# The first pair of a GeGLU MLP: x in pieces of 256 tokens by half of K, first half of K for all tokens first

## The chip, the cores and the metric

The kernel runs on one core of a Trainium2 chip. The time is the device time of one execution in microseconds (us); the traces place an instruction to some 0.1 us. TensorE is the matrix engine (PE in the profile, its weight loads PEld), VectorE is DVE, ScalarE is ACT, GpSimd is POOL; SPq is the queue on which SyncE issues the transfers.

## The reference

```python
# x: (8, 1024, 1024), w_gate, w_up: (1024, 4096), w_down: (4096, 1024), all fp32
gate = x @ w_gate
up = x @ w_up
gate = 0.5 * gate * (1 + tanh(sqrt(2 / pi) * (gate + 0.044715 * gate ** 3)))
out = (gate * up) @ w_down
```

## The kernel before

The kernel handles 1024 tokens at a time in eight passes, in fp16, with Strassen-like schemes of fewer products. In pass 0 nothing is prepared yet, so the first pair of column blocks (two blocks of 128 columns of gate and of up) is computed plainly: x is loaded in fp32, cast by VectorE, transposed by TensorE into PSUM, and copied out into four operands b11, b21 (first 512 tokens, two halves of K) and b12, b22 (the other 512 tokens). `mh` is the half of the tokens, `kh` the half of K, `g` a block of 128 tokens. Each load of x or of a weight block is 512 KB.

```python
def x0_load(mh, g):                       # 128 tokens, all of K: rows of 4 KB
    r0 = mh * MH + g * P
    nc.sync.dma_start(out=x0_f32[mh][:, g], in_=x2[r0 : r0 + P, :])

def x0_transpose(mh, g, b):
    ...                                   # eight 128x128 transposes into PSUM bank b
    nc.vector.tensor_copy(xq["b11" if mh == 0 else "b12"][:, :, c], ps[:, 0:KH])
    ...                                   # the other half of K is copied by ScalarE
# order of the loads:  x (mh 0) x4, weights of pair 0 x4, x (mh 1) x4, weights of pair 1 x4
...
def first_pair():
    ...
    warm(9)                               # matmuls on ones, to bring the clock up
    ...                                   # transposes of mh 0, each followed by warm(2) or warm(3)
    for kh in range(2):
        products(0, kh, slice(0, MH))
    ...                                   # casts and transposes of mh 1, first 256 tokens
    for kh in range(2):
        products(1, kh, slice(0, MQ))
    ...                                   # transposes of mh 1, other 256 tokens
    for w in range(2):
        cast_first(w, 1, slice(256, 512)) # last weight block of pair 1, on ScalarE
    for kh in range(2):
        products(1, kh, slice(MQ, MH))
    ...
    sum_x(1); sum_w(0, 1, 0); sum_w(0, 1, 1); sum_x(2)     # VectorE, for pair 1
    outputs(1, 0); outputs(1, 1)
    sum_x(3); sum_w(0, 1, 2); sum_w(0, 1, 3); sum_x(4)
```

Pair 1 is the next one. It starts with four products that need only x and its own weights (16 matmuls) and goes on with products of the sums.

## Time and profile before

| what | us | where it is read |
|---|---|---|
| median of six runs (2256.08 to 2257.9) | 2256.44 | times |
| span of the profiled run | 2254.4 | page |
| TensorE busy | 2246.1 | page, part 1 |
| first product of the first pair | 11.47 | timeline |
| first matmul of pair 1 | 28.72 | timeline |
| pair 1 comes to its last four products | 39.10 | timeline |
| last first-pair load lands | 27.3 | issue plus time to landing |
| wait of the matmuls at 279.69 | 0.43 | waits of TensorE |

A line of the timeline gives the start, the duration, the engine, the line of the program, the operation with what it writes and reads, how many instructions were merged, and in brackets how long the engine was idle before it and what ended that. Line numbers differ between the kernels: the first pair's products are L1198 before and L1206 after, pair 1 is L626 before and L635 after, the down projection L991 and L1000.

### The profile page before, as it was taken

How to read it: one execution, taken by the hardware profiler on the slowest of the kernel's cores; microseconds unless marked ns; L12 is line 12 of the kernel's file. 1: busy time of each engine (PE TensorE's matmuls, PEld its weight loads, DVE VectorE, ACT ScalarE, POOL GpSimd, SP SyncE). 2: the span in 40 equal slices, each digit the busy share in tenths (PEclk: the TensorE clock that was granted, in tenths of full speed). 3: DMA queues.
4: the chain of work that ended last, by engine and by line, in shares of the span. 5: the costliest groups of instructions: out<-in, count | busy, mean ns of one | idle time of the engine just before them, and what ended most of it. 6: DMA issues, size and time to landing. Idle time of an engine off the chain costs nothing.

```text
span 2254.4 us, 42805 instructions
## 1 busy us (share of the span) xinstructions
PE 2246.1 (100%) x16634; PEld 1625.6 (72%) x16634; DVE 1561.7 (69%) x2190; ACT 956.1 (42%) x1866; POOL 679.3 (30%) x825
## 2 busy tenths in 40 slices
PE   9999999999999999999999999999999999999999
PEld 4444444444444445888888888888888888888888
DVE  6576458883588755777776677666786667866674
ACT  4444135651355622666125550356404653055520
POOL 1332013330133200555014550255403543044520
PEclk9999999999999999999999999999999999999999
DMA  9898969989999999999998999989999889988876
GB/s 241 163 207 218 284 184 241 263 264 283 255 227 249 282 309 349 328 342 370 302 339 274 317 304 318 322 270 324 311 324 316 285 308 326 311 311 277 289 285 225
DMA packets 308093, 642.46 MB, mean 285 GB/s; under 512 B 79088, under 2 KB 185328, under 8 KB 287344
## 3 DMA queue, kind: packets, MB, share of 16 engines
q1 hardware_dynamic: 253104, 566.57, 73.2%
q0 software_dynamic: 54784, 73.14, 19.3%
q8 instruction: 130, 2.13, 0.4%
q14 instruction: 75, 0.61, 0.1%
HBM read 574.36 MB, written 138.41 MB: 316 GB/s over the span
## 4 chain that ended last, share of the span: by engine, by line
PE 87%; DMA 2%; SPq 0%; DVE 0%; issue 0%; DVEq 0%
PE ps L848 40%; PE ps L1099 20%; PE ps L626 17%; PE ps L991 10%; DMA wd_quads<-x_sums 1%; SPq L255 0%; DMA ring<-wd_ops 0%; DVE x_sums L452 0%; DVE h_a L923 0%; DVE tmp L1168 0%; DVE x_sums L278 0%; SPq L487 0%; DVEq L278 0%; SPq L535 0%
## 5 line engine op out<-in xcount | busy, mean ns | idle before, releaser
L848 PEld LDWEIGHTS <-ring 128*128 128x128 f16 x8320 | 814.1, 98 | 94.4
L825 POOL TENSOR_TENSOR h_a<-tmp 128x256 f16<-128x256 f32 x640 | 469.3, 753 | 839.3 <-ACT tmp L813 831.9
L848 PE MATMUL ps<-x_sums,ring 128*128 128x256 f16 x5760 | 655.8, 273 | 0.0
L810 DVE TENSOR_TENSOR tmp<-tmp,ps 128x512 f32<-128x512 f32 x640 | 414.5, 683 | 148.1 <-PE ps L848 99.7
L626 PEld LDWEIGHTS <-ring 128*128 128x128 f16 x2632 | 257.5, 98 | 310.4
L795 ACT COPY tmp<-ps 128x512 f32<-128x512 f32 x520 | 304.1, 585 | 237.5 <-PE ps L848 162.8
L626 PE MATMUL ps<-x_sums,ring 128*128 128x512 f16 x1504 | 339.8, 379 | 0.0
L813 ACT ACTIVATE tmp<-tmp 128x256 f32<-128x256 f32 x640 | 264.1, 418 | 172.8 <-DVE tmp L808 79.4
L848 PE MATMUL ps<-x_b,ring 128*128 128x256 f16 x2560 | 305.6, 273 | 0.0
L808 DVE TENSOR_TENSOR tmp<-ps,tmp 128x512 f32<-128x512 f32 x240 | 165.4, 689 | 145.2 <-ACT tmp L795 101.0
L626 PE MATMUL ps<-x_b,ring 128*128 128x512 f16 x1128 | 259.1, 379 | 0.0
L652 POOL TENSOR_TENSOR h_a<-tmp 128x512 f16<-128x512 f32 x94 | 144.5, 1537 | 374.8 <-ACT tmp L650 271.9
L1099 PEld LDWEIGHTS <-h_a 128*128 128x128 f16 x2240 | 219.2, 98 | 25.4
L991 PE MATMUL ps<-ring,h_a 128*128 128x512 f16 x1024 | 222.3, 379 | 0.4 <-DMA ring<-wd_ops 0.4
L1099 PE MATMUL ps<-ring,h_a 128*128 128x256 f16 x1920 | 216.1, 273 | 0.0
L991 PEld LDWEIGHTS <-h_a 128*128 128x128 f16 x1152 | 112.7, 98 | 136.6 <-DMA ring<-wd_ops 0.9
L645 DVE TENSOR_TENSOR tmp<-ps,tmp 128x512 f32<-128x512 f32 x188 | 127.2, 683 | 112.6 <-ACT tmp L637 111.1
L1156 ACT ACTIVATE tmp<-ps 128x512 f32<-128x512 f32 x60 | 35.3, 597 | 362.6 <-PE ps L1099 274.6
L1168 DVE SCALAR_TENSOR_TENSOR tmp<-ps,tmp 128x512 f32<-128x512 f32 x120 | 81.1, 690 | 97.5 <-PE ps L1099 66.6
L351 DVE TENSOR_TENSOR ring<-ring 128x1024 f16<-128x1024 f16 x188 | 138.7, 751 | 11.1 <-DMA ring<-in_w_up_dram 6.9
L637 ACT COPY tmp<-ps 128x512 f32<-128x512 f32 x188 | 109.9, 586 | 77.8 <-PE ps L626 77.8
L1099 PE MATMUL ps<-ring,x_sums 128*128 128x256 f16 x1120 | 126.3, 273 | 0.0
(102 smaller groups left out, 1532.0 us busy)
## 6 DMA issues: line engine op xcount, KB each, us to landing
ring<-w_ops SPq DMA_DIRECT2D x480, 512.0 KB, 5.0
ring<-wd_quads SPq DMA_DIRECT2D x110, 1024.0 KB, 7.0
ring<-wd_ops SPq DMA_DIRECT2D x35, 1024.0 KB, 8.2
out_dram<-tmp SPq DMA_DIRECT2D x128, 256.0 KB, 6.6
w_ops<-h_s SPq DMA_DIRECT2D x128, 256.0 KB, 6.7
ring<-in_w_gate_dram POOLq DMA_DIRECT2D x23, 1024.0 KB, 10.5
ring<-in_w_up_dram POOLq DMA_DIRECT2D x23, 1024.0 KB, 17.8
wd_quads<-x_sums SPq DMA_DIRECT2D x131, 128.0 KB, 6.4
```

What stands on the lines that cost most here:

```text
L351: nc.vector.tensor_tensor(o, a, b, op)
L626: nc.tensor.matmul(ps(b, w), lhs[:, k], rhs[:, k, :], start=(first and k == 0), stop=(k == KH - 1), skip_group_check=True,)
L645: nc.vector.tensor_tensor(o, ps("b", w), o, ADD)
L652: nc.gpsimd.tensor_tensor(hq[TO[n]][:, i, :], tmp[:, t[n, 1]], tmp[:, t[n, 0]], MUL)
L795: nc.scalar.copy(tmp[:, t[o[1]]], ps_all[:, bank[o[2]]])
L808: nc.vector.tensor_tensor(d, b, a, SUB)
L810: nc.vector.tensor_tensor(d, a, b, ADD if o[4] == "add" else SUB)
L813: nc.scalar.activation(d, d, GELU, scale=GSC)
L825: nc.gpsimd.tensor_tensor(h, tmp[:, t[o[1]], MQ : 2 * MQ], g, MUL)
L848: nc.tensor.matmul(ps_all[:, bank[c], w * MQ : (w + 1) * MQ], lhs[:, w, k], rhs[:, k], start=(first and w == 0 and k == 0), stop=(k == KH ...
L991: nc.tensor.matmul(ps_all[:, bank[b, g]], lhs[:, j, g * P : (g + 1) * P], dc[:, n, :], start=(first and j == 0), stop=(j == NP - 1), skip_ ...
L1099: nc.tensor.matmul(ps_all[:, bank[c], m * MQ : (m + 1) * MQ], lhs[:, j, m * P : (m + 1) * P], rhs[:, j, :], start=(first and j == 0 and m ...
```

## The change

The intent is to let TensorE begin real work earlier. x comes in pieces of 256 tokens by half of K, the first half of K for all tokens before the second, so that the first products need two pieces of x and one weight block instead of four and one. The transposes go through spare PSUM banks, the PSUM copies become one instruction of 1024 elements per piece, the first gate casts are split in two, and the warm-up shrinks from 18 matmuls to 12.

```diff
-    def x0_load(mh, g):
-        r0 = mh * MH + g * P
-        nc.sync.dma_start(out=x0_f32[mh][:, g], in_=x2[r0 : r0 + P, :])
+    def x0_load(mh, gp, kh):
+        r0 = mh * MH + gp * MQ
+        nc.sync.dma_start(
+            out=x0_piece(x0_f32[mh], gp, kh),
+            in_=x2[r0 : r0 + MQ, kh * KH * P : (kh + 1) * KH * P].rearrange("(t p) k -> p t k", p=P),
+        )
 ...
-        warm(9)
 ...
+        warm(7)
+        x0_cast(0, 0, 0)
+        x0_cast(0, 1, 0)
+        x0_transpose(0, 0, 0, 4, act)
+        warm(2)
+        x0_transpose(0, 1, 0, 5, dve)
+        warm(3)
+        halves(0)
+        cast_first(1, 0, c0, dve)
+        product(0, 0, 0, 0)
+        product(0, 0, 0, 1)
+        product(0, 0, 1, 0)
 ...          (the other pieces in the same manner)
+        for c in (lo, hi):
+            for w, j in ((0, 0), (0, 1), (1, 0)):
+                product(1, 1, w, j, c)
         for kh in range(2):
-            products(1, kh, slice(MQ, MH))
-
+            product(1, kh, 1, 1)
+        cast_first(0, 1, c1)
+        cast_first(1, 1, c1, dve)
         ps_free.clear()
-        ps_free.extend((0, 2, 1, 3, 4, 5, 6, 7))
+        ps_free.extend(range(8))
         sum_x(1)
 ...
+    for kh in range(2):
+        for gp in range(2):
+            x0_load(0, gp, kh)
+        for w in range(2):
+            load_first(w, kh, slice(0, 256))
+        for gp in range(2):
+            x0_load(1, gp, kh)
 ...          (then the four weight blocks of pair 1, as before)
```

More of the change, by code (lines that the diff above doesn't have):

```diff
@@ L290, with x0_piece, x0_cast, x0_transpose @@
     x0_f16 = hf["a12"].rearrange("p (t a) -> p t a", t=2 * G)
-    def x0_load(mh, g):
-        r0 = mh * MH + g * P
-        nc.sync.dma_start(out=x0_f32[mh][:, g], in_=x2[r0 : r0 + P, :])
-    def x0_cast(mh, g):
-        nc.vector.tensor_scalar(x0_f16[:, mh * G + g], x0_f32[mh][:, g], XSC, None, MUL)
-    def x0_transpose(mh, g, b):
-        h = x0_f16[:, mh * G + g]
-        ps = ps_all[:, b].bitcast(FP16).rearrange("p (k m) -> p k m", m=P)
-        for k in range(2 * KH):
-            nc.tensor.transpose(ps[:, k], h[:, k * P : (k + 1) * P], identity)
-        c = slice(g * P, (g + 1) * P)
-        nc.vector.tensor_copy(xq["b11" if mh == 0 else "b12"][:, :, c], ps[:, 0:KH])
-        if mh:
-            nc.scalar.copy(xq["b22"][:, :, c], ps[:, KH : 2 * KH])
-        else:
-            return lambda: nc.scalar.copy(xq["b21"][:, :, c], ps[:, KH : 2 * KH])
+    def x0_piece(t, gp, kh):
+        return t[:, 2 * gp : 2 * gp + 2, kh * KH * P : (kh + 1) * KH * P]
+    def x0_load(mh, gp, kh):
[4 more added lines that the diff above has]
+        )
+    def x0_cast(mh, gp, kh):
+        nc.vector.tensor_scalar(
+            x0_piece(x0_f16, 2 * mh + gp, kh), x0_piece(x0_f32[mh], gp, kh), XSC, None, MUL
+        )
+    def x0_transpose(mh, gp, kh, b, copy):
+        h = x0_piece(x0_f16, 2 * mh + gp, kh)
+        ps = ps_all[:, b].bitcast(FP16).rearrange("p (k m) -> p k m", m=MQ)
+        o = xq[f"b{kh + 1}{mh + 1}"][:, :, gp * MQ : (gp + 1) * MQ]
+        for k in range(KH):
+            for t in range(2):
+                nc.tensor.transpose(
+                    ps[:, k, t * P : (t + 1) * P], h[:, t, k * P : (k + 1) * P], identity
+                )
+        copy(o, ps)
     def raw(p, q):
@@ L328, in load_first, with cast_first @@
         )
-    def cast_first(w, kh, cols, copy=nc.scalar.copy):
-        copy(raw(0, 0)[:, w, kh * KH : (kh + 1) * KH, cols], staging0(w, kh)[:, :, cols])
+    def cast_first(w, kh, cols, copy=nc.scalar.copy, ks=slice(0, KH)):
+        o = raw(0, 0)[:, w, kh * KH : (kh + 1) * KH, cols]
+        copy(o[:, ks], staging0(w, kh)[:, ks, cols])
     def load_raw(p, q):
@@ L1192, in first_pair, with product @@
         bank = {(mh, j, w): 4 * mh + 2 * j + w for mh in range(2) for j in range(2) for w in range(2)}
-        def products(mh, kh, c):
-            for w in range(2):
-                for j in range(2):
-                    for k in range(KH):
-                        nc.tensor.matmul(
-                            ps_all[:, bank[mh, j, w], c],
-                            raw(0, 0)[:, w, kh * KH + k, j * P : (j + 1) * P],
-                            xq[f"b{kh + 1}{mh + 1}"][:, k, c],
-                            start=(kh == 0 and k == 0 and c.start == 0),
-                            stop=(kh == 1 and k == KH - 1),
-                            skip_group_check=True,
-                        )
+        full, lo, hi = slice(0, MH), slice(0, MQ), slice(MQ, MH)
+        def product(mh, kh, w, j, c=full):
+            for k in range(KH):
+                nc.tensor.matmul(
+                    ps_all[:, bank[mh, j, w], c],
+                    raw(0, 0)[:, w, kh * KH + k, j * P : (j + 1) * P],
+                    xq[f"b{kh + 1}{mh + 1}"][:, k, c],
+                    start=(kh == 0 and k == 0 and c.start == 0),
+                    stop=(kh == 1 and k == KH - 1),
+                    skip_group_check=True,
+                )
         def outputs(mh, j):
@@ L1223, in first_pair @@
         nc.scalar.activation(mark, hf["s3"][:, 0:1], GELU)
-        for g in range(G):
-            x0_cast(0, g)
-        warm(9)
-        late = []
-        for g in range(G):
-            late.append(x0_transpose(0, g, 4 + g))
-            warm(2 if g < G - 1 else 3)
-        for w in range(2):
-            cast_first(w, 0, slice(0, 256))
-        for f in late:
-            f()
-        for w in range(2):
-            cast_first(w, 1, slice(0, 256), nc.vector.tensor_copy)
-        for kh in range(2):
-            products(0, kh, slice(0, MH))
@@ L1240, in first_pair, with halves @@
-        for g in range(2):
-            x0_cast(1, g)
-        for g in range(2):
-            x0_transpose(1, g, 6 + g)
-        for g in range(2, G):
-            x0_cast(1, g)
-        outputs(0, 0)
-        for w in range(2):
-            cast_first(w, 0, slice(256, 512))
+        dve, act = nc.vector.tensor_copy, nc.scalar.copy
+        c0, c1 = slice(0, 256), slice(256, 512)
+        def halves(kh):
+            for ks in (slice(0, 2), slice(2, 4)):
+                cast_first(0, kh, c0, act, ks)
@@ new lines, in first_pair @@
+        warm(7)
[10 more added lines that the diff above has]
+        product(0, 0, 1, 0)
+        x0_cast(1, 0, 0)
+        x0_transpose(1, 0, 0, 6, act)
+        product(0, 0, 1, 1)
+        x0_cast(1, 1, 0)
+        x0_transpose(1, 1, 0, 7, dve)
+        for c in (lo, hi):
+            for j in range(2):
+                product(1, 0, 0, j, c)
@@ new lines, in first_pair @@
+        x0_cast(0, 0, 1)
+        x0_transpose(0, 0, 1, 5, act)
+        x0_cast(0, 1, 1)
+        x0_transpose(0, 1, 1, 7, dve)
+        halves(1)
+        product(1, 0, 1, 0)
+        cast_first(1, 1, c0, dve)
+        product(0, 1, 0, 0)
+        product(0, 1, 0, 1)
+        x0_cast(1, 0, 1)
+        x0_transpose(1, 0, 1, 7, act)
+        x0_cast(1, 1, 1)
+        product(0, 1, 1, 0)
+        product(0, 1, 1, 1)
+        x0_transpose(1, 1, 1, 7, dve)
+        outputs(0, 0)
+        outputs(0, 1)
@@ L1250, in first_pair @@
+        for w in range(2):
+            cast_first(w, 0, c1)
         nc.gpsimd.tensor_copy(mark, staging0(1, 0)[:, 0, 256:257])
         load_raw(0, 1)
+        for c in (lo, hi):
+            for w, j in ((0, 0), (0, 1), (1, 0)):
+                product(1, 1, w, j, c)
         for kh in range(2):
-            products(1, kh, slice(0, MQ))
-        for g in range(2, G):
-            x0_transpose(1, g, g - 2)
-        outputs(0, 1)
-        for w in range(2):
-            cast_first(w, 1, slice(256, 512))
@@ L1259, in first_pair @@
-        for kh in range(2):
-            products(1, kh, slice(MQ, MH))
+            product(1, kh, 1, 1)
+        cast_first(0, 1, c1)
+        cast_first(1, 1, c1, dve)
         ps_free.clear()
-        ps_free.extend((0, 2, 1, 3, 4, 5, 6, 7))
+        ps_free.extend(range(8))
         sum_x(1)
@@ L1273, in first_pair @@
         sum_x(4)
-    for g in range(G):
-        x0_load(0, g)
-    for c in (slice(0, 256), slice(256, 512)):
-        for kh in range(2):
-            for w in range(2):
-                load_first(w, kh, c)
-        if c.start == 0:
-            for g in range(G):
-                x0_load(1, g)
+    for kh in range(2):
[5 more added lines that the diff above has]
+            x0_load(1, gp, kh)
+    for kh in range(2):
+        for w in range(2):
+            load_first(w, kh, slice(256, 512))
     for p in range(NPASS):
```

## The prediction

> **What bounds the kernel now.** I first read the busy table of the page: TensorE is busy for all but 8 us of the span, so only a shorter TensorE stream or a smaller gap in it can help. The change touches only the first pair of column blocks, so I then read the timeline of the first 37 us. The columns are start, duration, engine, line, operation, and in brackets what the engine waited for.
>
> ```profile
> PE 2246.1 (100%) x16634; PEld 1625.6 (72%) x16634; DVE 1561.7 (69%) x2190; ACT 956.1 (42%) x1866; POOL 679.3 (30%) x825
> ...
> 11.47 7.23 PE L1198 MATMUL ps<-x_b,ring 128*128 128x512 f16 x32 [0.59 <-ACT ring L331]
> 20.17 3.65 PE L1198 MATMUL ps<-x_b,ring 128*128 128x256 f16 x32 [0.58 <-DVE x_b L305]
> 25.23 3.65 PE L1198 MATMUL ps<-x_b,ring 128*128 128x256 f16 x32 [0.52 <-DVE x_b L305]
> 28.72 3.63 PE L626 MATMUL ps<-x_b,ring 128*128 128x512 f16 x16
> ```
>
> The first pair's own products take 7.23 + 3.65 + 3.65 = 14.5 us and its 64 transposes about 4.2 us (16 of them take 1.06 us), together 18.7 us; yet pair 1 (L626) starts at 28.72 us. The rest, 10 us, is warm-up matmuls and gaps, because nothing can be multiplied before 11.47 us. From 28.72 us to 200 us TensorE shows no gap at all.
>
> Next, what the beginning is fed by. In the timeline, the starts of the casts follow the landings of the 512 KB loads:
>
> ```profile
> 10.37 1.05 ACT L331 CAST ring<-x_sums 128x1024 f16<-128x1024 f32 x1 [8.13 <-DMA x_sums<-in_w_gate_dram]
> 12.04 1.05 ACT L331 CAST ring<-x_sums 128x1024 f16<-128x1024 f32 x1 [0.63 <-DMA x_sums<-in_w_up_dram]
> 13.54 0.69 DVE L331 CAST ring<-h_a 128x1024 f16<-128x1024 f32 x1 [2.67 <-DMA h_a<-in_w_gate_dram]
> 15.03 0.69 DVE L331 CAST ring<-h_a 128x1024 f16<-128x1024 f32 x1 [0.80 <-DMA h_a<-in_w_up_dram]
> 16.31 0.69 DVE L297 TENSOR_SCALAR h_a<-h_a 128x1024 f16<-128x1024 f32 x1 [0.58 <-DMA h_a<-in_x_dram]
> 17.59 0.69 DVE L297 TENSOR_SCALAR h_a<-h_a 128x1024 f16<-128x1024 f32 x1 [0.58 <-DMA h_a<-in_x_dram]
> ```
>
> A weight block comes every 1.50 us, a block of x every 1.28 us: the loads form one stream without pauses. Of the last of the 16 loads, the timeline gives the issue, the view of DMA issues the time to landing (11.0 us), so it lands at 27.3 us.
>
> ```profile
> 16.32 2.15 SPq L326 DMA_DIRECT2D h_a<-in_w_up_dram  x1
> ...
> h_a<-in_w_up_dram SPq DMA_DIRECT2D x1, 512.0 KB, 11.0
> ```
>
> Last, what VectorE does when that load is there: the sums that pair 1 needs, one after another until 36.18 us.
>
> ```profile
> 27.68 1.22 DVE L267 TENSOR_TENSOR x_sums<-x_b,x_b 128x2048 f16<-128x2048 f16 x1
> 28.95 1.42 DVE L351 TENSOR_TENSOR ring<-ring 128x1024 f16<-128x1024 f16 x2
> 30.29 1.22 DVE L267 TENSOR_TENSOR x_sums<-x_b,x_sums 128x2048 f16<-128x2048 f16 x1
> 31.42 1.28 DVE L1211 TENSOR_TENSOR h_a<-ps,tmp 128x512 f16<-128x512 f32 x2
> 32.62 1.22 DVE L267 TENSOR_TENSOR x_sums<-x_b,x_b 128x2048 f16<-128x2048 f16 x1
> 33.75 1.29 DVE L351 TENSOR_TENSOR ring<-ring 128x1024 f16<-128x1024 f16 x2
> 34.96 1.22 DVE L267 TENSOR_TENSOR x_sums<-x_b,x_sums 128x2048 f16<-128x2048 f16 x1
> ```
>
> **What the Trainium skill says.** "DMA: Bandwidth & Descriptors", section "Why small descriptors are slow (HBM only)": every packet carries a fixed overhead, so small ones are slower. The trace agrees: of 16 DMA engines each moves 32 packets of 1 KB of a weight block in 1.50 us (46.9 ns each) and 8 packets of 4 KB of an x block in 1.28 us (160 ns each); a straight line through both has a fixed part of 9 ns. The same page, "Queues, rings and completion order": one copy is split over up to 16 rings and a later one may complete unevenly across engines. The trace agrees: in the windows the DMA share falls to 0.10 from 25 to 26 us, though the last load lands at 27.3, so a straggling engine sets the landing. "VectorE: DVE Perf Modes", section "The perf-mode tier table": a 16-bit tensor_tensor of 2048 elements is capped at 2x (1224 ns); the trace has 1.22 us, so the sums cannot shrink. "TensorE: Matmul & The Clock Gate", section "What's actually happening": cold matmuls run at half rate for a window of some 3.4 us. The trace agrees: the first warm-up weights are 0.43 us apart, L626's matmuls 0.217 us; the change keeps 12 of 18 warm-ups.
>
> **The change part by part.** *Loads.* x comes in rows of 2 KB in place of 4 KB. By the straight line a 2 KB packet takes 84.6 ns, 16 of them per engine 1.35 us: 0.07 us more per load, 8 x loads, 0.5 to 0.6 us in all. The last four loads (the weights of pair 1) keep their order, so the last one lands at about 27.8 us in place of 27.3. Estimated landings, taking over the 0.95 us irregularity that the third load shows now: x 4.1, 5.45; gate 7.9; up 9.4; x (second half of the tokens) 10.75, 12.1; x (second half of K) 13.45, 14.8; gate 16.3; up 17.8; x 19.15, 20.5.
>
> *TensorE.* A product of four 512-column matmuls takes 0.87 us (16 in 3.47), one of 256 columns 0.114 us (32 in 3.65), eight transposes 0.53 us. The first product now waits for two x pieces and half a gate cast: 7.9 + 0.6 = 8.5 us instead of 11.47. Three products of gate and up run to 11.1; two transposes with the fourth product and the 16 small matmuls wait for x at 10.75 and 12.1 plus 0.69 for the cast, ending at 15.5. Transposes of the second half of K wait for VectorE (casts queue behind a PSUM copy) until about 16.8, and the seventh product ends at 17.7. Gate at 16.3 is there, but ScalarE first has a 1.05 us PSUM copy; two products to 19.6; transposes at 19.9, two products to 22.2, transposes to 22.8, then 24 small matmuls (2.75) and four of the last products' halves (1.74): 27.3 us. So TensorE would reach pair 1 some 1.4 us earlier than 28.72, with three or four gaps of 0.2 to 0.5 us left. Removing six warm-ups is worth nothing by itself; they lay in gaps.
>
> *VectorE after the last load.* Here is the point where I chose. The order of instructions in the changed kernel puts the cast of the last weight block on VectorE, ahead of the first sum. So the chain of sums starts at 27.8 + 0.69 = 28.5 us, against 27.68 now: 0.8 us later. With today's offsets its results come at: second x sum 28.5 + 3.83 = 32.3; third weight sum 28.5 + 6.75 = 35.25; fourth x sum 28.5 + 8.5 = 37.0. Pair 1 needs them 5, 8 and 10 products after its start (4.33, 6.93 and 8.66 us). Its start counts as no earlier than 32.3 - 4.33 = 28.0, 35.25 - 6.93 = 28.3, 37.0 - 8.66 = 28.35. Today's slack there is 37.4 - 36.2 = 1.2 us; the change uses it up.
>
> *Sum.* TensorE gets to pair 1 at 27.3 but loses about 1 us inside it: effectively 28.35 against 28.72, a gain of 0.4 us. All later work is unchanged apart from bank numbers, and 2256.2 - 0.4 = 2255.8 us.
>
> **The rivals.** *Full gain.* If the last load lands near 26.3 (14 engines look done by 25 us; the straggler may not recur), VectorE is early and TensorE's own 1.4 us, or up to 1.8 if the x loads are not slower, reach the end: 2254.4 to 2254.8. Against it: the loads are slower by packet size. *Loss.* If the straggler hits a later x piece, or VectorE's cast comes at 28.5, the sums end after 37.7 and the kernel is 0.5 us slower: 2256.7. For it: the cast heads the chain of seven steps and nothing reorders it. *Swallowed later.* The only gap in the matmuls up to 300 us is at 279.7 us, behind a load:
>
> ```profile
> 279.69 20.68 PE L991 MATMUL ps<-ring,h_a 128*128 128x512 f16 x95 [0.43 <-DMA ring<-wd_ops]
> ```
>
> If that load does not come earlier, 0.4 us vanish there: 2256.2. Against it: the chain of waits leads from it back to VectorE at 231 us, which had started after TensorE's last products of the pass, so it should move along.
>
> **Range and chances.** The middle lies between these: 2255.8 us. The three runs before spread over 1.8 us by themselves, and the rivals reach from 2254.4 to 2256.7; with noise I take 2254.2 to 2257.2. A change of 2% would be 45 us, more than the whole first pair: within 2% 0.985, faster 0.008, slower 0.007.
>
> **What would show it.** Right: first products at about 8.5 us; x loads of 2 KB spaced 1.35 us; TensorE reaching pair 1 near 27.3 us; new waits of pair 1 on VectorE's sums, about 1 us together; the last load at 27.8. Wrong: no waits of pair 1 on VectorE and a gain of over 1 us (last load early); or the first product after 10 us (landing order not as I read it); or a longer gap than 0.43 us near 280 us that takes the gain. A change above 3 us would mean that a later stage depends on the new bank order, which I see no reason for.

## The result, and the profile after

The changed kernel takes 2255.45 us, median of six runs (2254.61 to 2256.63), against 2256.44 for the kernel before in the same rounds. The ratio of the two is 0.9995 with a 95% interval of 0.9982 to 1.0008. A ratio is computed as the mean time of one kernel's fast runs over that of the other's of the same rounds, so it is not quite the ratio of the medians. By the times alone the two kernels are the same. A second session (below) gave 2255.07 (2254.65 to 2255.63, five runs) against 2256.74 (2255.90 to 2257.79, nine runs): the two groups do not overlap there, but the interval of the ratio, 0.9980 to 1.0005, still holds 1. What was gained, if it is a gain, is of the order of 1 us.

The trace shows where it comes from. This is the timeline of TensorE in the changed kernel:

```profile
9.29 3.35 PE L1206 MATMUL ps<-x_b,ring 128*128 128x512 f16 x12
...
27.31 3.62 PE L635 MATMUL ps<-x_b,ring 128*128 128x512 f16 x16
30.77 3.73 PE L635 MATMUL ps<-x_sums,ring 128*128 128x512 f16 x16
34.68 3.64 PE L635 MATMUL ps<-x_sums,ring 128*128 128x512 f16 x16 [0.19 <-DVE ring L360]
38.16 3.62 PE L635 MATMUL ps<-x_b,ring 128*128 128x512 f16 x16
```

And this is the line of the kernel before that answers to the last one:

```profile
39.10 3.62 PE L626 MATMUL ps<-x_b,ring 128*128 128x512 f16 x16
```

The first products start 2.2 us earlier (9.29 against 11.47), pair 1 starts 1.41 us earlier (27.31 against 28.72), and at its last four products the lead is 0.94 us (38.16 against 39.10). So 0.47 us were lost inside pair 1. The starts of the single matmuls show where: the fifth of the second line comes 0.12 us late and the first of the third line 0.35 us late, both released by VectorE; before the fourth line there is no wait.

This is VectorE's timeline in the changed kernel at that place:

```profile
27.40 0.69 DVE L340 CAST ring<-h_a 128x1024 f16<-128x1024 f32 x1 [2.27 <-DMA h_a<-in_w_up_dram]
28.01 1.22 DVE L267 TENSOR_TENSOR x_sums<-x_b,x_b 128x2048 f16<-128x2048 f16 x1
...
33.94 1.29 DVE L360 TENSOR_TENSOR ring<-ring 128x1024 f16<-128x1024 f16 x2
35.14 1.22 DVE L267 TENSOR_TENSOR x_sums<-x_b,x_sums 128x2048 f16<-128x2048 f16 x1
```

It stands idle for 2.27 us until the last weight block lands at 27.40 us, casts it, and only then begins the sums. They end at 36.36 us, 0.18 us later than before; TensorE, which came 1.41 us earlier, now runs into them.

The bandwidth of the transfers near the end of the loads shows in the windows (busy time of PE, PEld, DVE, ACT, POOL with counts; granted clock, DMA share, GB/s). Before and after:

```profile
25.00:26.00 1.00, 0.77 (x8) 0.68 (x8) 0.18 (x1) 1.00 (x3) 0.82 (x1) 1.00 0.10 35
```

```profile
25.00:26.00 1.00, 1.00 (x9) 0.71 (x8) 0.13 (x1) 0.62 (x1) 0.78 (x1) 1.00 0.46 145
```

After the change most engines still move data between 25 and 26 us (share 0.46 against 0.10), yet the last load lands at 27.40 us, against 27.3 before.

Last, the load that the matmuls near 279 us wait for:

```profile
278.93 6.43 PE L1000 MATMUL ps<-ring,h_a 128*128 128x512 f16 x29 [0.60 <-DMA ring<-wd_ops]
```

They start 0.76 us earlier than before (279.69), with a wait of 0.60 instead of 0.43 us: of the lead of 0.94 us, 0.17 is lost there. From there on the two traces run in parallel, and the spans differ by 0.8 us (2253.6 against 2254.4).

### The profile page after: what moved, and what is told of

It reads as the page before. It is cut to its first block, busy times and chain, and to the rows that moved or that the text cites. A ratio compares the mean times of both kernels' runs of the same rounds, so it can differ in the third digit from the quotient of the medians.

```text
span 2253.6 us, 42764 instructions
## 1 busy us (share of the span) xinstructions
PE 2245.6 (100%) x16616; PEld 1624.2 (72%) x16616; DVE 1565.1 (69%) x2187; ACT 955.4 (42%) x1863; POOL 674.6 (30%) x825
## 4 chain that ended last, share of the span: by engine, by line
PE 87%; DMA 2%; SPq 1%; DVE 0%; issue 0%; DVEq 0%
PE ps L857 40%; PE ps L1108 20%; PE ps L635 17%; PE ps L1000 10%; DMA wd_quads<-x_sums 1%; SPq L255 0%; DMA ring<-wd_ops 0%; DVE x_sums L278 0%; DVE h_a L932 0%; DVE tmp L1177 0%; SPq L496 0%; DVEq L278 0%; SPq L544 0%
```

## The experiments

My theory was: VectorE's chain after the last landing limits pair 1, TensorE's own lead is larger, and what is left of the lead reaches the end. The rivals were that TensorE's arrival alone decides, that the late clock at the start costs time at the end, and that the load near 279 us swallows gains.

**1. The x sums ahead of the last cast** (edit of the changed kernel)

```diff
         cast_first(0, 1, c1)
+        sum_x(1)
+        sum_x(2)
         cast_first(1, 1, c1, dve)
         ...
-        sum_x(1)
         sum_w(0, 1, 0)
         sum_w(0, 1, 1)
-        sum_x(2)
```

> The changed kernel with the first two x sums of VectorE put ahead of its cast of the last weight block; they need no part of that block. Theory (VectorE's chain after the last landing limits pair 1): in the changed kernel VectorE is idle from 25.1 to 27.4 us, so two sums of 1.22 us fit there, its last x sum ends near 34.5 us instead of 36.4, the two short waits of pair 1 on VectorE vanish, and the last sixteen matmuls of pair 1 that read x_b start at 37.7 us instead of 38.16: about 0.45 us earlier, and the span about 0.4 us shorter than that of the changed kernel (2253.2 against 2253.6). Rival (TensorE's arrival at pair 1 alone decides, the waits were noise of the trace): 38.1 to 38.2 as before. Rival (the gate near 279 us swallows): earlier at 38 us but the matmuls behind the load at 279 us start at 278.9 all the same, with a longer wait.

Timeline of VectorE, then of TensorE:

```profile
25.04 1.22 DVE L267 TENSOR_TENSOR x_sums<-x_b,x_b 128x2048 f16<-128x2048 f16 x1
26.29 1.23 DVE L267 TENSOR_TENSOR x_sums<-x_b,x_sums 128x2048 f16<-128x2048 f16 x1
27.59 0.69 DVE L340 CAST ring<-h_a 128x1024 f16<-128x1024 f32 x1
```

```profile
27.31 3.62 PE L635 MATMUL ps<-x_b,ring 128*128 128x512 f16 x16
30.76 7.07 PE L635 MATMUL ps<-x_sums,ring 128*128 128x512 f16 x32
```

The two sums fill VectorE's idle time, the 32 matmuls on sums run in one piece without a gap, and the last four products start at 37.67 us, 0.49 us earlier than in the changed kernel. TensorE arrived at 27.31 us in both, so its arrival alone did not decide: the chain on VectorE cost what the trace suggested. The matmuls behind the load near 279 us start at 278.36 us, 0.57 us earlier than in the changed kernel, so that load did not swallow the gain here. The span is 2253.0, the median of four runs 2254.54 us.

**2. Nine warm-up matmuls instead of seven** (edit of the changed kernel: `warm(7)` becomes `warm(9)`)

> The changed kernel with nine warm-up matmuls at the start, as in the kernel before, in place of seven. Theory (the idle 0.72 us ahead of the first transposes moved the clock's step from 7.6 to 10.7 us): full clock again near 7.6 us, the first twelve products take 2.6 us instead of 3.35, TensorE reaches pair 1 about 0.4 to 0.5 us earlier (26.9 instead of 27.3); but VectorE's sums still end at 36.4, so the waits of pair 1 grow by the same amount and the x_b matmuls start at 38.1 again: span within 0.15 us of the changed kernel's. Rival (the early clock costs time at the end): they start at 37.7 and the span is 0.4 us shorter. Rival (clock is not tied to those two matmuls): full clock still at about 10.7 us.

Timeline of TensorE and of VectorE:

```profile
8.54 2.75 PE L1206 MATMUL ps<-x_b,ring 128*128 128x512 f16 x12
```

```profile
21.70 0.69 DVE L304 TENSOR_SCALAR h_a<-h_a 128x1024 f16<-128x1024 f32 x1 [2.14 <-DMA h_a<-in_x_dram]
```

Half of it came as expected: the first products start at 8.54 us instead of 9.29 and take 2.75 us instead of 3.35. But TensorE came to pair 1 at 27.25 us, not at 26.9, and the matmuls on x_b started at 38.27. The early lead was lost at the last piece of x: its cast began at 21.70 us here and at 20.44 in the changed kernel. The rival, that the early clock costs time at the end, wanted the x_b matmuls at 37.7 us and is not supported; but since the late x piece sits between, this run does not rule it out. The span, expected within 0.15 us of the changed kernel's 2253.6, was 2252.9: this expectation failed, because no wait stood near 279 us. The median of four runs is 2255.79 us.

That the two warm-up matmuls alone decide when the clock steps up is not shown, either. The trace of experiment 4, which has seven of them like the changed kernel, runs the first eight transposes at full rate already (0.62 us, against 1.03 in the changed kernel), and its products start as early as here:

```profile
5.54 0.62 PE L314 MATMUL ps<-identity,h_a 128*128 128x128 f16 x8 [0.93 <-DVE h_a L304]
8.37 2.85 PE L1206 MATMUL ps<-x_b,ring 128*128 128x512 f16 x12 [0.18 <-ACT ring L340]
```

By the trace's own record the full clock comes at 10.49 us in the changed kernel, at 8.97 to 10.64 in four other traces with the same seven warm-up matmuls, at 4.32 in experiment 4 and at 4.40 in experiment 7, which splits them; in the five traces with nine it comes between 4.74 and 7.38. So a late step went with seven warm-up matmuls in five traces of six. That is a tendency and not a rule, and the 0.72 us of idle time in my theory do not explain it (0.93 in experiment 4).

**3. Both edits**

> Both edits: x sums ahead of the last cast, and nine warm-up matmuls. Theory: with VectorE out of the way, the earlier arrival counts: pair 1 at 26.9 us, no wait inside it, the x_b matmuls at 37.3 us, 0.85 us earlier than the changed kernel and 1.8 earlier than the kernel before (39.10); span 2252.8, if the load near 279 us moves along. Rival (that load is held by transfers, not by TensorE): the gap there grows from 0.6 to over 1.2 us and the span stays near 2253.5.

My number failed: the matmuls on x_b start at 37.89 us instead of 37.3. No gap is left in pair 1 (27.53 plus 10.36 us of matmuls is 37.89), but TensorE arrived only at 27.53, because the last x piece again landed late (21.98 us). There was no wait near 279 us, and that brought the span to the expected 2252.8 by luck, in spite of the late arrival; the rival about that load is not supported. The median is 2254.92 us, not distinguishable from that of experiment 1.

**4. The last cast on ScalarE** (edit of the changed kernel: `cast_first(1, 1, c1, dve)` becomes `cast_first(1, 1, c1)`)

> The changed kernel with the cast of the last weight block on ScalarE, as in the kernel before, in place of VectorE. Theory: the first x sum then needs nothing and runs at 25.1 us; the weight sums wait for the ScalarE cast, which takes 1.05 us from 27.4 (28.45); the last x sum ends near 35.9 us, just early enough, and the gain is the same 0.4 us as in the run with the sums moved. Rival (the cast on VectorE is harmless, only the landing counts): no change, 38.16.

Both expectations failed: the matmuls on x_b started later than in the changed kernel, at 38.81 us (span 2254.4; median of four runs 2255.90 us, against 2254.54 for experiment 1 in the same rounds). Timeline of ScalarE, then of TensorE:

```profile
27.61 1.04 ACT L340 CAST ring<-h_a 128x1024 f16<-128x1024 f32 x1 [0.33 <-DMA h_a<-in_w_up_dram]
28.57 1.08 ACT L1218 ACTIVATE tmp<-ps 128x512 f32<-128x512 f32 x2
29.53 1.08 ACT L651 COPY ps<-ps 128x512 f32<-128x512 f32 x2
```

```profile
30.18 1.89 PE L635 MATMUL ps<-x_b,ring 128*128 128x512 f16 x8 [0.94 <-ACT ps L651]
```

The cast holds up two activations and with them the PSUM copies (L651) that the third product of pair 1 accumulates onto. I had followed the cast to VectorE's sums and not to what stands behind it on ScalarE. VectorE's chain no longer held TensorE up, as expected, but a new wait of 0.94 us took its place. Between the two engines, neither has room for the last cast in front of its other work; the order of experiment 1 makes the room.

**5. A delay in the kernel before** (`warm(16)` is added ahead of `ps_free.clear()` in the first pair)

> The kernel before with sixteen more matmuls on ones at the end of the first pair: TensorE comes to pair 1 3.47 us later, all else is the same. If everything later is paced by TensorE (theory), the matmuls at 279.69 us move by 3.4 to 3.5 us to 283.1 with a wait of 0.3 to 0.6 us, and the span grows by 3.4 to 3.5 us to 2257.8. If the load near 279 us is held by transfers that do not wait for TensorE (rival), the wait of 0.43 us vanishes and the span grows by 3.0 us only; then any gain in the first pair is lost there.

TensorE came to pair 1 at 32.62 us, 3.90 us later than before; some 3.45 us are the added matmuls. The rest was there before the edit had any part: the first loads landed later in this run (the third one was complete at 8.13 us instead of 7.56), and so the first product started at 12.06 us. Near 284 us:

```profile
284.69 0.60 PE L991 MATMUL ps<-ring,h_a 128*128 128x512 f16 x2 [1.53 <-DMA ring<-wd_ops]
```

The wait neither vanished nor stayed: it grew to 1.53 us, and the end came 4.99 us later (2255.09 against 2250.10 in the chains of waits). So the load is not anchored in time; it moves along with TensorE. My number for the span (2257.8) missed by 1.6 us. The wait is one reason. Another is the trace that it is held against: a run of the kernel before in the same round as this one had a span of 2255.8 instead of 2254.4, and against that the growth is 3.6 us, close to the expected 3.4 to 3.5. With one run of each, only the direction can be read: the load moves with TensorE.

**6. Only the size of the x pieces, in the kernel before**

```diff
     def x0_load(mh, g):
-        r0 = mh * MH + g * P
-        nc.sync.dma_start(out=x0_f32[mh][:, g], in_=x2[r0 : r0 + P, :])
+        gp, kh = divmod(g, 2)
+        r0, c = mh * MH + gp * MQ, slice(kh * KH * P, (kh + 1) * KH * P)
+        nc.sync.dma_start(
+            out=x0_f32[mh][:, 2 * gp : 2 * gp + 2, c],
+            in_=x2[r0 : r0 + MQ, c].rearrange("(t p) k -> p t k", p=P),
+        )
```

> The kernel before, only its x loads cut into pieces of 256 tokens by half of K (2 KB rows, eight loads of 512 KB as before). Prediction's step: each x load takes 1.35 us instead of 1.28, so fourteen of the sixteen transfer engines end 0.5 to 0.8 us later (DMA share in the window from 25 to 26 us 0.4 instead of 0.10) and the last load lands 0.5 us later, at 27.8. Rival, from the changed kernel's trace: the end is set by the straggling engine, and with 2 KB rows the straggling at the start (0.65 us) does not occur, so the last load lands at 27.3 to 27.5 as before. Pair 1 moves with TensorE, whose first products wait for the casts of whole rows: 28.7 to 29.4 us.

The window of this run:

```profile
25.00:26.00 1.00, 0.48 (x8) 0.34 (x6) 0.69 (x2) 0.70 (x2) 1.00 (x2) 1.00 0.80 254
```

The share of 0.80 says that the mass of the transfers ends much later. The trace also records each transfer engine's completion of each load: fourteen of the sixteen finish the last load at 25.40 us before, 26.46 here and 26.24 in the changed kernel, the slowest at 27.27, 27.50 and 27.38. So smaller rows delay the mass by 1.06 us, more than the 0.5 to 0.8 I expected, but the last landing by only 0.23 us: the rival is right. Of the 1.06 us, 0.75 are there at the first load already (fourteen engines at 4.62 us against 3.87); that part is not a sum of slower loads. The first x piece lands later, too: its completion record is at 4.00 us before, at 4.66 here and 4.70 in the changed kernel. At 29.25 us TensorE comes to pair 1 0.53 us late, because the casts wait for two pieces; there was no wait near 279 us, and the span, 2254.3, ended up the same. A gain of half a microsecond can thus be made or lost at 279 us by that wait alone.

**7. More TensorE instructions ahead** (edit of experiment 1: each of the first seven warm-up matmuls is split into four of 128 columns)

Experiments 2 and 3 raised the question why the last x piece lands at 20.4 us in some runs and at 21.7 to 22.0 in others. In the traces a single transfer of the kind "instruction", 16 KB and 1.1 to 1.2 us long, comes between 19.1 and 22.8 us. It starts at 19.12 us in run 2, 19.53 in run 1, 19.78 in run 3 and 19.31 in run 4, where the piece is late (21.79 us in run 4), and at 20.28 in the changed kernel, where it is not. The traces of experiment 8 agree: 20.02 to 20.55 us, and the piece on time in all three.

> The run with the x sums moved, and each of the first seven warm-up matmuls split in four of 128 columns: 42 more TensorE instructions, about the same TensorE time. Theory (the 16 KB instruction transfer near 20 us is TensorE's, comes after a fixed number of its instructions, and holds up one transfer engine by over 1 us): it comes several us earlier, between 13 and 18 us, and every load after it lands late on one engine: the last x piece at 21.7 us as in the run without the split, the last weight block again near 27.5. Rival (the transfer comes at a fixed time or belongs to another engine): it stays between 19.3 and 20.6 us.

The view of DMA between 17 and 18 us, then VectorE's timeline:

```profile
q8 instruction: 1, 0.02, 7.2%
```

```profile
19.35 0.69 DVE L340 CAST ring<-h_a 128x1024 f16<-128x1024 f32 x1 [2.58 <-DMA h_a<-in_w_up_dram]
20.55 0.69 DVE L304 TENSOR_SCALAR h_a<-h_a 128x1024 f16<-128x1024 f32 x1 [0.51 <-DMA h_a<-in_x_dram]
21.94 0.69 DVE L304 TENSOR_SCALAR h_a<-h_a 128x1024 f16<-128x1024 f32 x1 [0.70 <-DMA h_a<-in_x_dram]
```

The transfer came at 17.13 us, and now the up block of the first pair (19.35 us, against 17.75 in the changed kernel) and all loads after it are late, the last x piece at 21.94. Since only TensorE's instructions were added, this supports that the transfer feeds TensorE, and that it holds up the one engine that carries it. It is one run. TensorE ran early in it (its twelve products after the sixteen transposes start at 16.68 us), but so it did in experiments 2 and 4 (16.52 and 16.62), where the transfer came at 19.12 and 19.31; the added instructions brought it forward by 2 us more. TensorE had started 116 of its matmuls by then, against 103 to 106 in the eight other traces of this order, so the number is nearly fixed, not strictly.

The scatter of the start has a pattern, too. In those eight traces the transfer starts 2.36 to 2.69 us after the same twelve products, which start between 16.52 and 18.08 us. So it follows TensorE: where TensorE runs early, the transfer comes before the last x piece is complete and that piece lands late, which is how the early lead of experiment 2 was lost. This is read from eight traces, not tested by itself.

**8. Three kernels with five rounds on one chip:** the changed kernel, experiment 1, and experiment 1 with the load of the 279 us matmuls issued ahead of the transposing transfers. The edit of the last one:

```diff
-                    if nb == 0 and g == 0 and p + 1 < NPASS:
+                    if nb == (1 if p == 0 else 0) and g == 0 and p + 1 < NPASS:
                         ...
                         transpose_x(p + 1)
```

> The changed kernel once more, for a comparison of medians on one chip with the next two: 2255.5 us, within its earlier spread of 2254.6 to 2256.6.

> The run with the x sums ahead of the last cast, once more. Theory: its matmuls of pair 1 on x_b start 0.45 to 0.5 us before those of the changed kernel, and the median is 0.4 to 0.9 us lower (2254.5 to 2255.1), the scatter of the wait near 279 us (0 to 0.7 us in the traces) being as large.

> The same, and in the first down projection the four transposing transfers of the next x are issued one block later, so that the load that the matmuls near 279 us wait for goes ahead of them on the queue (in the traces it is issued at 270 to 271.6 us, right behind 10 to 12 us of transposing transfers). Theory (that wait is a matter of queue order, and it alone scatters between 0 and 1.5 us): no wait there, span 0.5 us shorter than with the sums moved (2252.5), median near 2254.1 and a smaller spread. Rival (bandwidth holds that load, not order): a wait of 0.3 us or more stays there, or comes up at the scaling of the next x at the end of the down projection, near 306 us.

| kernel | median, us | lowest to highest |
|---|---|---|
| before (nine runs) | 2256.74 | 2255.90 to 2257.79 |
| changed | 2255.07 | 2254.65 to 2255.63 |
| x sums first | 2254.70 | 2254.09 to 2255.45 |
| x sums first, load ahead | 2254.19 | 2254.17 to 2254.74 |

The timeline of SyncE's queue in the last kernel, then of TensorE:

```profile
258.77 0.40 SPq L544 DMA_DIRECT2D ring<-wd_ops  x1
259.22 14.20 SPq L255 DMA_TRANSPOSE x_b<-x_half  x4
```

```profile
277.69 20.88 PE L1000 MATMUL ps<-ring,h_a 128*128 128x512 f16 x96
```

The load goes out at 258.77 us instead of 270.35, and no wait stands before the matmuls. Four of the eleven other traces show none there either, so this one trace does not prove the theory; the smaller spread of the five times (0.57 us against 1.36) speaks for it, weakly. No wait came up at the scaling of the next x either, but another of 0.4 us did, much later, on a VectorE tile, so the span is 2252.9 and not 2252.5. The second trace of experiment 1 also shows no wait there, by luck (span 2252.3); single spans do not rank these two. The matmuls of experiment 1 on x_b started at 37.58 us, 0.66 us before the 38.24 of the changed kernel and not 0.45 to 0.5. The reason is that TensorE arrived at 27.22 instead of 27.64 us; inside pair 1 the changed kernel lost only 0.24 us in this second trace, half of what it lost in the first.

The second trace also tells what sets this point in the changed kernel. In the three traces that have the last cast on VectorE ahead of the sums, TensorE arrives at pair 1 at 27.31, 27.64 and 27.25 us (experiment 2), but the x_b matmuls start 10.76, 10.76 and 10.75 us after that cast begins (27.40, 27.48 and 27.52). The last landing and VectorE's chain set it, not TensorE's arrival.

In the medians the three versions lie in the expected order, 0.4 and 0.5 us apart, with overlapping ranges; all three lie wholly below the kernel before. The last one, 2.55 us below it in the median, is the best version found.

## Why the prediction was right or wrong

The predicted time, 2255.8 us, lies 0.35 us above the measured 2255.45, inside the range, and "within 2%" was right. That says little: the whole first pair is shorter than 2%. The predicted gain was 0.4 us; measured were 0.8 us between the spans of the two traces and 1.0 us between the medians, within the noise of the times. So the test of the prediction is in its steps.

- *First product at about 8.5 us*: it came at 9.29. The step that failed was leaving the rate of TensorE out: the last warm-up matmuls still ran at half rate and held the products up until 9.29 us. The window of some 3.4 us that I quoted does not describe these traces: in them the full clock came 2.7 to 9 us after the first warm-up matmul. Two more of them, in experiment 2, had the products at 8.54, but experiment 4 had them at 8.37 with seven, so their number alone is not shown to be the cause. A cost at the end could not be shown.
- *x loads 1.35 us apart*: right. The casts that follow two pieces start at 10.65 and 12.00 us.
- *TensorE at pair 1 near 27.3 us*: 27.31. The time is right, the way there only in part: TensorE was 0.8 us behind my schedule at the start, 0.4 at the transposes of 20.34 us (I had 19.9) and 0.3 at those of 22.52 (22.2); at the end I had allowed a little too much for the last transposes and products. Two errors in the landings had cancelled: the first two x pieces were complete at 4.70 and 6.01 us (estimated 4.1 and 5.45), the gate block at 7.76 (7.9), because the irregularity of the third load that I carried along did not recur.
- *The last load at 27.8 us*: wrong, 27.40. The landing is set by the slowest engine, and I added the delay of the mass to a landing that the slowest engine had set, carrying its present irregularities along: that step failed. It landed 0.11 us later than before (27.38 against 27.27 in the completion records). The delay of the mass was 0.84 us, against 0.5 to 0.6, but only in part for my reason: 0.70 us of it are there at the first load (fourteen engines at 4.57 us against 3.87), and from the first load to the last the mass took 0.14 us longer. And in both kernels the slowest engine falls furthest behind at the first load that lands after the instruction transfer of experiment 7 (20.69 us before, 20.28 after): from 0.6 to 2.0 us behind the fourteenth before, from 0.3 to 1.2 after.
- *Pair 1 waits for VectorE about 1 us*: the mechanism was right and is shown by experiment 1; the size was 0.47 us (0.24 in the second trace), since the chain started at 28.01 us and not at 28.5. That is the mis-sized term: the gain at the last products of pair 1 was predicted at 0.4 us and measured at 0.94. The waits came after five and eight products, as predicted; the third one, after ten, did not occur.
- *Swallowed later*: I expected the load near 280 us to move along. It did, within a fraction: 0.17 of 0.94 us was lost there. In experiment 5 it followed TensorE; but over the twelve traces the wait scatters from 0 to 1.53 us, as much as the gain itself. What makes it scatter was not found; issued ahead of the transposing transfers the load caused no wait in the one trace taken.

What stays open: whether the early clock would count if the last x piece were on time, what decides when the clock steps up, and which part of the change brought TensorE's 1.41 us. Only the piece size was tried alone (experiment 6), and it brought TensorE to pair 1 0.53 us later.

## What to carry to other kernels

When an engine is made to arrive earlier, look at what it meets: here a quarter to half a microsecond of a lead of 1.1 to 1.4 us went into sums on VectorE that stood, by their order, behind a cast waiting for the last load, though two of them did not need it. Put what needs nothing ahead of what waits. And where a load is complete only when the slowest of sixteen engines is, do not add a delay of the mass to a landing that one straggler sets.

## What the Trainium skill lacked or had wrong

- "DMA: Bandwidth & Descriptors", "Bandwidth": it has sizes of whole transfers for the GpSimd path, but no time per row size for loads from SyncE. Here, loads of 512 KB came every 1.50 us in rows of 1 KB, 1.35 in rows of 2 KB and 1.28 in rows of 4 KB; with rows of 2 KB the first load of the program completed at 4.66 to 5.32 us in ten traces, with rows of 4 KB at 3.96 and 4.00 in two.
- The same page, "Queues, rings and completion order", says that engines alternate between rows, but not what that costs a load; nor does "Instruction fetch mechanics" in "Runtime: NRT & Kernel Launch". Here one instruction transfer of 16 KB (1.1 to 1.2 us, listed under queue 8) went with landings that were 1.3 to 1.6 us late for the x piece or weight block behind it.
- "TensorE: Matmul & The Clock Gate", "Part 4: PE-mode transpose", gives some 275 ns for a transpose in a kernel. As a latency that is near the 242 ns mean of the transposes' records in the changed kernel; in a row, sixteen of them took 1.06 us, 66 ns each.
